# A hybrid short-conv and gated-delta step: the first group prepares the heads' weights ahead of its convolutions

## The chip, the cores and the metric

One Trainium2 chip, one of its cores. The metric is the device time in microseconds (us) of one execution of the whole program. TensorE is called PE here, VectorE DVE, ScalarE ACT, GpSimd POOL, and SyncE, which issues all DMA transfers, SP.

## What is computed

One step of one encoder layer over a prompt of 4096 rows and a sample of 32 rows, 1024 wide:

```python
h    = rmsnorm(x, ln_pre)
proj = h @ w_in          # 4104 columns: B_a | C_a | X_a | Z_a | qkv | Z_g | decay, beta
# group A, 512 channels: short gated conv
y_a  = B_a * conv3_causal(C_a * X_a) * silu(Z_a)
# group B, 4 heads of 128: gated delta rule
q, k, v = silu(conv4_causal(qkv));  q, k L2-normalised
S_t  = exp(g_t) (I - beta_t k_t k_t^T) S_{t-1} + beta_t k_t v_t^T;   o_t = q_t^T S_t / sqrt(dk)
y_g  = rmsnorm_head(o) * silu(Z_g)
y    = x + rmsnorm(concat(y_a, y_g) @ w_out, ln_post)
```

Outputs are y for the prompt and the sample, and the new convolution histories and states of both.

## The kernel before

The prompt is cut into 16 blocks of 256 rows. The program runs in three stages: sixteen groups in which the projection of the heads' columns, their convolutions and the delta rule are computed (to about 1360 us), then the columns of group A for all rows, then the product with `w_out`. Group 0 holds the sample and block 0, and is written by `first_group`; groups 1 to 15 hold one block each.

The columns of `w_in` are taken in tiles of 128, and the tiles in pairs. Tiles 16 to 19 are q, 20 to 23 k, 24 to 27 v, 28 to 31 Z_g, and the 8 columns of tile 32 the gates; group A has 0 to 15. A pair is named here by its first tile. Group 0 takes the eight pairs in the order 20, 22, 16, 18, 24, 26, 28, 30 (`steps`, L857).

Before a pair can be used, its weights are prepared by `prep_b` (L722), which does the following for the two tiles:

- load each tile, 128 x 1024 numbers of 4 bytes, 0.52 MB, from HBM (L205). Tiles 20 and 21 go to buffers of tag `v`, 22 and 23 to buffers of tag `zg`, all the others to the five buffers of tag `xt` (`NXT`, L33), which the rows of x use too;
- multiply by `ln_pre` (L206), on POOL, for tile 20 on DVE; take the absolute value (L208, ACT), sum it over the rows by products with ones (`rL`, PE), and make a power of two for each column out of it (L223, L224, L229, L230, DVE);
- multiply the tile by it (L232, DVE), turn the scales into a column (`ou`, PE; L239, DVE) and scale the convolution's weights `cw` (L732, DVE);
- cut the tile into two halves of 16 bits: the high one on ACT (L728), the low one on POOL, for tile 21 on DVE (L729). With L729 the tile's buffer is free again, and SP can load another into it.

With both halves there, PE projects the sample and block 0 (`pjs_c` and `pj_c`), ACT takes the result out (`us`, `u`), and DVE convolves it (L436: `qks` and `qk`). `pair` does this for one pair of tiles and one block. The norm of x, its transposes and its cut into halves are in `xprep` (L271 to L299); the convolution's old rows of the sample come from `cache_conv_qkv` (L836, copied by DVE in L840 to `hq`).

Behind the convolutions of a block come the decays (L321 to L399) and the matrices of the two chunks (`stage1`), then a triangular substitution, `subst` (L525 to L573): its right side is set up by DVE (L539 to L541), the 31 steps run on POOL for a block of the prompt (`la`, `lt`, from L546 on) and on DVE for the sample (`hllts`), and DVE transposes the result (L556). From group 1 on `prep_a` prepares a pair of group A's weights beside each block: its loads go to the same five buffers, and its L206 is on DVE.

The order on the engines is not written by hand. A scheduler takes every instruction with a priority, the place at which it was written, and sets each engine's order and SP's order of transfers by it and by its own model of time; on the chip each engine, and SP too, works through its list in that order. `first(fn, *a)` runs `fn` with a priority raised by 1500 places, so that what it writes is put ahead of what was written up to 1500 places before it, where its inputs allow:

```python
for si, (kind, c0) in enumerate(steps):
    ...
    for kd_, c_ in steps[:si + 1 + (AH if si >= AS else 0)]:
        ct = (28 if kd_ == "z" else 16) + c_
        if ct not in W:
            prep_b(ct)
```

`AH` is 1 and `AS` 5: up to the step of pair 24 a pair is prepared in its own step, then one step early. Pair 20 is prepared outside this loop.

Of the kernel before, what the change touches and what calls it, by code (L numbers as in the profile page):

```python
# [41 lines left out]
def bc(ap, axis, n):  # L42

    shape = list(ap.shape)
    shape.insert(axis, n)
    return ap.unsqueeze(axis).to_broadcast(shape)
# [3 lines left out]
def hybrid_kernel(  # L50
# [112 lines left out]
    def w_tile(ct):  # L163
        i = 2 * b_order.index(ct)
        return tuple(w_slot(i + x, [P, KT, P], F16, ct) for x in range(2))
# [16 lines left out]
    def te(shape, dtype, tag, bufs=1, nm=""):  # L182
        return pe.tile(shape, dtype, tag=tag, bufs=bufs, name=f"{tag}{nm}")
# [201 lines left out]
    def in_turn(steps):  # L385

        steps = list(steps)
        while steps:
            steps = [s for s in steps if next(s, steps) is None]

    def decays(b):

        C, nch, E3 = b["C"], b["nch"], b["E3"]
        nr = nch * NH
        sfx = "s" if b["s"] else ""
        gB = te([P, nr, C + 1], F32, "gB" + sfx, 1, b["id"])
        dma(gB, b["gd"].unsqueeze(0).to_broadcast([P, nr, C + 1]))
        V.tensor_tensor(E3[:, 0], gB[:, :, C - 1], gB[:, :, C], ALU.subtract)

        def exps():  # L400
            if C < P:
                A.activation(E3[:, 0], E3[:, 0], AF.Exp)
                return A.activation(E3[:C, 1:3], E3[:C, 1:3], AF.Exp)
            return A.activation(E3[:, 0:3], E3[:, 0:3], AF.Exp)
        queued("exp", exps)
        E = gB[:C, :, :C]
        for c in range(nch):
            for i in range(c * NH, (c + 1) * NH):
                V.scalar_tensor_tensor(E[:, i], E[:, i], E3[:C, 3, i:i + 1], mneg[:C, :C], ALU.subtract, ALU.min)
            queued("exp", lambda: A.activation(E[:, c * NH:(c + 1) * NH], E[:, c * NH:(c + 1) * NH], AF.Exp))  # L410
        b["E"] = E
# [37 lines left out]
    def pair(b, kind, c0):  # L449
        n = b["n"]  # L450
        if kind == "z":
            return z_pair(b, c0)
        if kind == "v":
            return qkv_pair(b, c0, b["v"][:, c0 - 8:c0 - 6, :n])
        h0 = c0 % 4
        return qkv_pair(b, c0, b["qk"][:, h0:h0 + 2, 0 if kind == "k" else 1, :n])
# [42 lines left out]
    def stage1(b, c):  # L499
        norm_qk(b, c, 0)  # L500
        norm_qk(b, c, 1)
        gram(b, c)

    def rnorms(b):
        C, nch = b["C"], b["nch"]
        r = te([P, 2, 2, NH], F32, "r", 2, b["id"])[:C, :nch]
        rf = r.rearrange("p c x h -> p (c x h)")
        sf = b["ss"].rearrange("p c x h -> p (c x h)")
        V.tensor_scalar(sf, sf, EPS, None, ALU.add)
        rsqrt(sf, rf)  # L510
        sm = tl([P, 5, 2, NH], F32, "sm", 3, b["id"])[:C, :, :nch]
        rk, rq = r[:, :, 0], r[:, :, 1]
        br, nb_, nbe, cc, c2 = (sm[:, i] for i in range(5))
        V.tensor_tensor(br, b["beta"], rk, ALU.mult)
        V.scalar_tensor_tensor(nb_, br, -1.0, rk, ALU.mult, ALU.mult)
        V.tensor_tensor(nbe, nb_, b["e1"], ALU.mult)
        V.tensor_scalar(cc, rq, P ** -0.5, None, ALU.mult)
        V.scalar_tensor_tensor(c2, cc, 1.0 / P, cc, ALU.mult, ALU.mult)
        b.update(br=br, nb_=nb_, nbe=nbe, cc=cc, c2=c2)
# [190 lines left out]
    def setup_block(b):  # L710
        b["nch"] = b["n"] // b["C"]
        b["qk"] = tl([P, NH, 2, NB1], F32, "qk", 3, b["id"])
        if b["s"]:
            b["v"], b["zg"] = (te([P, NH, NS], F32, x, 1, "s") for x in ("vs", "zgs"))
        else:
            b["v"], b["zg"] = (tl([P, NH, NB1], F32, x, 2, b["id"]) for x in ("v", "zg"))
        b["hist_new"] = te([P, 12, 3], F32, "hists" if b["s"] else "hist", 2 if b["s"] else 3, b["id"])
        b["ss"] = te([P, 2, 2, NH], F32, "ss", 2, b["id"])[:b["C"], :b["nch"]]
        nb = b["C"] // 32
        b["lad"] = dp.tile([2, NH, 4, 32, 32], F32, tag=f"lad{nb}", bufs=2, name=f"lad{b['id']}")[:b["nch"], :, :nb]  # L720
        b["kd"], b["M"], b["at"], b["rec"] = [], [], [], {}

    def prep_b(ct):

        in_turn([scaled((ct, ct + 1))])
        for i, w in enumerate(wa["w"]):
            hi, lo = W[ct + i] = w_tile(ct + i)
            A.activation(hi, w, AF.Copy)  # L728
            (V if ct + i in VLO else G).tensor_tensor(lo, w, hi, ALU.subtract)  # L729
        if ct < 28:  # L730
            c = ct - 16
            V.tensor_tensor(cw[:, :, c:c + 2], cw[:, :, c:c + 2], bc(usc[:, ct:ct + 2], 1, 4), ALU.mult)  # L732
# [67 lines left out]
    def init_hist(b, ct):  # L800

        c = ct - 16
        inv = te([P, 2], I32, "inv", 2, f"{ct}")
        V.tensor_scalar(inv, usc[:, ct:ct + 2].bitcast(I32), -1, float(254 * BIT), ALU.mult, ALU.add)
        V.tensor_tensor(b["hist"][:, c:c + 2], hq[:, :, c:c + 2].rearrange("p j c -> p c j"),
                        bc(inv.bitcast(F32), 2, 3), ALU.mult)
# [63 lines left out]
    def first(fn, *a):  # L870

        with tc.high_priority(1500):
            fn(*a)

    def ends(gen):
        for _ in gen:
            pass
# [20 lines left out]
    def first_group(grp):  # L898

        for b in grp:  # L900
            setup_block(b)
            if b["s"]:
                b["hist"] = te([P, 12, 3], F32, "hists", 2, "i")
                state[1] = te([P, NH, P], F32, "hl", 4, "s0")
                dma(state[1], state_gdn[0, 0].rearrange("h k v -> k h v"))
        for si, (kind, c0) in enumerate(steps):
            if si == 4:
                in_turn([gates(b) for b in grp])
                for b in grp:
                    decays(b)  # L910
            for kd_, c_ in steps[:si + 1 + (AH if si >= AS else 0)]:
                ct = (28 if kd_ == "z" else 16) + c_
                if ct not in W:
                    prep_b(ct)
            if kind != "z":
                init_hist(smp, 16 + c0)
            for b in grp:
                ends(pair(b, kind, c0))
            if si == 6:
                xprep(groups[1][0])  # L920
            if si in (4, 5):
                for b in grp:
                    if si - 4 < b["nch"]:
                        stage1(b, si - 4)
            if si == 5:
                for b in grp:
                    rnorms(b)
                    subst(b)
            if si == 7:
                in_turn([gates(groups[1][0])])  # L930

    prevs = []
    for gi, grp in enumerate(groups):
        b, s0 = grp[-1], 16 * gi
        if gi == 0:
            first_group(grp)
            for p in grp:
                finish(p, s0)
# [452 lines left out]
```

## Time and profile before

| | |
|---|---|
| three runs | 2382.73, 2385.70 and 2390.21 us (median 2385.7) |
| the profiled execution | 2385.77 us, of which the span from the first to the last instruction is 2384.1 us |
| mean granted clock of PE | 0.956 of full speed |
| busy, share of the span | PE 90%, PE's weight load 72%, DVE 66%, ACT 41%, POOL 56% |
| DMA moved | 230.81 MB, 97 GB/s over the span |

The profile is one execution. All times of instructions are in us from the start of its span. A line such as L232 is the line of the kernel; DVE times are shown with what the engine sat idle for just ahead of the instruction, in brackets with what ended that wait.

### The profile page before, as it was taken

The numbers are of one execution on the slowest core, as the hardware profiler recorded it, in microseconds if no ns is written. First come the engines' busy times: TensorE is split into PE (matmuls) and PEld (weight loads), VectorE is DVE, ScalarE is ACT, GpSimd is POOL, SyncE is SP. The second block draws the span as 40 slices with busy tenths as digits, with TensorE's granted clock in tenths as the row PEclk, the third lists the DMA queues.
The fourth block names the chain that finished last, engine by engine and source line by source line (L and its number), as shares of the span: only waits on it lengthen the run. The fifth ranks groups of instructions, "written<-read, shape, count | busy, mean of one in ns | idle before, by whom it ended". The sixth has DMA issues, their size and how long they took to land. (4 is left out here: it accounts for less than half of the span.)

```text
span 2384.1 us, 48173 instructions
## 1 busy us (share of the span) xinstructions
PE 2141.4 (90%) x18626; PEld 1713.9 (72%) x18626; DVE 1564.8 (66%) x3720; ACT 980.3 (41%) x2513; POOL 1333.7 (56%) x1750
## 2 busy tenths in 40 slices
PE   4676989799889988998899999899999999999998
PEld 3465878687778777877778889788888888444443
DVE  4786877677777786767766655656576656455661
ACT  4454655465556555655565411121221121333331
POOL 4435573656675767566776430674467431466763
PEclk9788999899899999999999999999999999999999
DMA  6344341433334243433342425212211122344441
GB/s 125 46 104 92 87 114 48 78 105 97 91 91 111 87 101 87 115 92 95 80 123 72 148 112 182 84 63 71 89 46 54 45 92 88 113 159 145 136 135 72
DMA packets 257198, 230.81 MB, mean 97 GB/s; under 512 B 111576, under 2 KB 196376, under 8 KB 256968
## 3 DMA queue, kind: packets, MB, share of 16 engines
q1 hardware_dynamic: 256968, 227.73, 33.9%
q8 instruction: 146, 2.39, 0.4%
q14 instruction: 84, 0.69, 0.1%
HBM read 133.09 MB, written 76.74 MB: 88 GB/s over the span
## 5 line engine op out<-in xcount | busy, mean ns | idle before, releaser
L74 PEld LDWEIGHTS <-w 128*128 128x128 f16 x6528 | 624.8, 101 | 117.7 <-POOL w L729 16.9
L74 PE MATMUL pj_c<-hhi,w 128*128 128x256 f16 x3072 | 559.6, 282 | 3.0 <-ACT u L430 3.0
L74 PE MATMUL pj_c<-hlo,w 128*128 128x256 f16 x1536 | 433.4, 282 | 0.0
L74 PEld LDWEIGHTS <-w_a 128*128 128x128 f16 x2880 | 269.5, 98 | 48.0 <-issue 16.0
L74 PEld LDWEIGHTS <-opm 128*128 128x128 f16 x1536 | 149.3, 98 | 176.2 <-issue 0.7
L551 POOL TENSOR_TENSOR lt<-lt 128x112 f32<-128x112 f32 (+29 forms) x496 | 235.4, 475 | 37.0
L436 DVE SCALAR_TENSOR_TENSOR qk<-u,cw,qk 128x256 f32<-128x256 f32 x384 | 238.5, 667 | 9.5 <-ACT qk L434 9.1
L550 POOL TENSOR_TENSOR lt<-la,lt 128x112 f32<-128x112 f32 (+29 forms) x496 | 211.6, 427 | 36.2
L74 PE MATMUL pja<-op,w_a 128*128 128x256 f16 x1536 | 190.0, 273 | 3.1 <-DVE w L1034 1.9
L74 PE MATMUL pj_z<-hhi,w 128*128 128x256 f16 x1024 | 187.9, 281 | 0.0
L74 PE MATMUL ga<-op,w_a 128*128 128x256 f16 x1152 | 147.7, 274 | 10.5 <-DVE w L1034 6.7
L74 PE MATMUL pj_z<-hlo,w 128*128 128x256 f16 x512 | 144.0, 281 | 0.0
L74 PE MATMUL pjo<-w_o,opm 128*128 128x512 f16 x528 | 118.5, 379 | 0.0
L137 POOL TENSOR_TENSOR oss<-oss,mhalf 128x2 f32<-128x2 f32 (+1 forms) x17 | 50.0, 2940 | 114.6 <-DVE oss L1280 114.6
L74 PE MATMUL ro<-w_o,opm 128*128 128x512 f16 x504 | 113.4, 379 | 0.0
L74 PE MATMUL go<-w_o,opm 128*128 128x512 f16 x504 | 113.1, 379 | 0.0
L546 POOL TENSOR_TENSOR la<-la,lt 128x1024 f32<-128x1024 f32 x16 | 38.0, 2374 | 126.9 <-DVE lt L541 103.6
L1034 DVE TENSOR_TENSOR w<-pja,w 128x256 f32<-128x256 f32 x152 | 61.7, 420 | 63.6 <-PE pja L74 61.5
L769 ACT ACTIVATE op<-tsc 128x512 f16<-128x512 f32 x48 | 30.2, 630 | 173.0 <-POOL tsc L775 100.0
L750 POOL TENSOR_TENSOR hl<-xtw,hl 128x512 f16<-128x512 f32 x56 | 66.7, 1208 | 61.9 <-ACT hl L749 61.9
L436 DVE SCALAR_TENSOR_TENSOR v<-u,cw,v 128x256 f32<-128x256 f32 x192 | 98.6, 549 | 3.0 <-ACT v L434 2.8
L437 ACT ACTIVATE qk<-qk 128x512 f32<-128x512 f32 x64 | 40.2, 633 | 142.8 <-DVE qk L436 142.8
(650 smaller groups left out, 4791.4 us busy)
## 6 DMA issues: line engine op xcount, KB each, us to landing
xt<-in_x_prompt_dram SPq DMA_DIRECT2D x32, 512.0 KB
mx<-mxd SPq DMA_DIRECT2D x16, 1024.0 KB
op<-hTd SPq DMA_DIRECT2D x30, 512.0 KB
xtw<-in_w_in_dram SPq DMA_DIRECT2D x28, 512.0 KB
wad<-hl SPq DMA_DIRECT2D x56, 256.0 KB
gB<-gd SPq DMA_DIRECT2D x16, 516.0 KB
hTd<-hhi SPq DMA_DIRECT2D x16, 512.0 KB
hTd<-hlo SPq DMA_DIRECT2D x16, 512.0 KB
```

Source lines behind the costliest of these rows:

```text
L74: return self.queue(nc.tensor.matmul(*a, **k))
L137: G.tensor_tensor(y, x, mhalf[:x.shape[0], :x.shape[-1]], ALU.pow)
L436: V.scalar_tensor_tensor(d, u[:, i, j:j + n], cw[:, j, c0 + i:c0 + i + 1], d, ALU.mult, ALU.add)
L437: queued("silu", lambda: A.activation(dst, dst, AF.Silu))
L546: E.tensor_tensor(la, la, bc(rl, 1, 32), ALU.mult)
L550: E.tensor_tensor(tm, bc(la[:, j, j + 1:32], 2, w), bc(lt[:, j, 0:w], 1, r), ALU.mult)
L551: last = E.tensor_tensor(lt[:, j + 1:32, 0:w], lt[:, j + 1:32, 0:w], tm, ALU.subtract)
L750: G.tensor_tensor(hl[:, 1], src, hl[:, 0], ALU.subtract)
L769: A.activation(d[i][0], t, AF.Copy)
L1034: V.tensor_tensor(dst, p, src, ALU.add)
```

## The change

```diff
@@ first_group
             for kd_, c_ in steps[:si + 1 + (AH if si >= AS else 0)]:
                 ct = (28 if kd_ == "z" else 16) + c_
                 if ct not in W:
-                    prep_b(ct)
+                    first(prep_b, ct)
             if kind != "z":
                 init_hist(smp, 16 + c0)
```

No instruction is added or taken away. The preparation of the pairs 22, 16, 18, 24, 26, 28 and 30 gets the raised priority; that of pair 20 does not pass here. The scheduler makes another order of it on all engines up to about the third group, and the same order as before in the second and third stage.

On SP, at the program's start, the loads stood like this (`vw` are tiles 20 and 21, `zgw` 22 and 23, `xtw_628` and `xtw_641` 16 and 17, `xtw_287` the gates' columns, `hls` the state, `hTds` is a write of the sample's x):

```order
L123 DMA lnp<-in_ln_pre_dram 128x8x1
L266 DMA xts_153<-in_x_sample_dram 32x1024
L828 DMA wecst<-in_conv_qkv_w_dram 48x128
L205 DMA vw_183<-in_w_in_dram 128x8x128
L205 DMA vw_196<-in_w_in_dram 128x8x128
L266 DMA xt_0_232<-in_x_prompt_dram 128x1024
```

and now stand like this:

```order
L205 DMA zgw_453<-in_w_in_dram 128x8x128
L205 DMA zgw_466<-in_w_in_dram 128x8x128
L123 DMA lnp<-in_ln_pre_dram 128x8x1
L266 DMA xts_153<-in_x_sample_dram 32x1024
L828 DMA wecst<-in_conv_qkv_w_dram 48x128
L205 DMA vw_183<-in_w_in_dram 128x8x128
```

The two loads of pair 22 went from behind `hls` to the front; a little later the load of tile 16 also passed `hls`, and that of tile 17 the two writes `hTds`.

On POOL the difference at the start is (`L137` is the power of -1/2 in the norm of x, `w_20` the low half of tile 20):

```order
+L206 TENSOR_TENSOR zgw_453<-zgw_453,lnp 128x1024
+L206 TENSOR_TENSOR zgw_466<-zgw_466,lnp 128x1024
 L137 TENSOR_TENSOR xsss<-xsss,mhalf 32x1
 L206 TENSOR_TENSOR vw_196<-vw_196,lnp 128x1024
 L206 TENSOR_TENSOR xtw_287<-xtw_287,lnp 128x8x8
+L206 TENSOR_TENSOR xtw_628<-xtw_628,lnp 128x1024
 L137 TENSOR_TENSOR xss_231<-xss_231,mhalf 128x2
-L206 TENSOR_TENSOR zgw_453<-zgw_453,lnp 128x1024
-L206 TENSOR_TENSOR zgw_466<-zgw_466,lnp 128x1024
-L206 TENSOR_TENSOR xtw_628<-xtw_628,lnp 128x1024
+L206 TENSOR_TENSOR xtw_641<-xtw_641,lnp 128x1024
 L729 TENSOR_TENSOR w_20_221<-vw_183,w_20_220 128x1024
```

The multiplications of pair 22 and of tiles 16 and 17 moved up, past the norm of x of the sample, past that of block 0, and past the low half of tile 20.

On DVE the rows around the scaling of pair 16 (`xtw_628`, `xtw_641`) were before (`qk_318` are block 0's convolutions of pair 20, `qks` the sample's of pair 22):

```order
L436 SCALAR_TENSOR_TENSOR qk_318<-u_4_438,cw,qk_318 128x256 x6
L429 COPY u_6_613<-histi 128x2x3
L223 TENSOR_SCALAR we_627<-rL_626 128x256
L224 TENSOR_SCALAR we_627<-we_627 128x256
L229 TENSOR_SCALAR wu_656<-we_627 1x256
L230 TENSOR_SCALAR we_627<-we_627 128x256
L431 COPY histss<-us_551 128x6
L232 TENSOR_TENSOR xtw_628<-xtw_628,we_627 128x1024
L436 SCALAR_TENSOR_TENSOR qks<-us_551,cw,qks 128x32
L232 TENSOR_TENSOR xtw_641<-xtw_641,we_627 128x1024
```

and are now:

```order
L230 TENSOR_SCALAR we_627<-we_627 128x256
L325 TENSOR_TENSOR gzs<-gzs,dtb 32x4
L328 TENSOR_SCALAR gexs<-gzs 32x4
L323 TENSOR_TENSOR gz_1038<-g_1036 128x16
L232 TENSOR_TENSOR xtw_628<-xtw_628,we_627 128x1024
L232 TENSOR_TENSOR xtw_641<-xtw_641,we_627 128x1024
L327 SCALAR_TENSOR_TENSOR gexs<-gzs 32x4
L239 COPY usc<-ou_661 128x2
L324 TENSOR_TENSOR gz_1038<-gz_1038,ug 128x16
L436 SCALAR_TENSOR_TENSOR qk_318<-u_4_438,cw,qk_318 128x256 x2
```

The scaling of pair 16 stands ahead of the convolutions of pair 20 instead of behind them, and the later pairs likewise, each ahead of the convolutions that it followed. Further on, the two L206 of `prep_a` in group 1 (`xtw_2559`, `xtw_2567`) stood behind L539 to L541 of block 0's substitution on DVE, and now stand ahead of them.

## Rows read from the trace of the kernel before

**Rows 1.** Busy time of each engine by stretch, with PE's granted clock and the DMA rate
```profile
core 0: us, PE busy (x) PEld busy (x) DVE busy (x) ACT busy (x) POOL busy (x), PEclk, DMA share, GB/s
0.00:50.00 50.00, 20.37 (x177) 16.66 (x178) 19.05 (x57) 21.75 (x33) 20.02 (x27) 1.00 0.69 138
50.00:100.00 50.00, 31.93 (x390) 25.91 (x388) 40.34 (x91) 19.82 (x35) 20.73 (x11) 0.73 0.35 52
100.00:150.00 50.00, 34.73 (x391) 28.25 (x390) 43.43 (x124) 28.34 (x66) 26.28 (x18) 0.83 0.34 70
150.00:200.00 50.00, 37.34 (x351) 31.67 (x349) 39.15 (x115) 25.77 (x74) 19.54 (x25) 0.85 0.61 122
200.00:250.00 50.00, 39.67 (x337) 32.80 (x337) 31.82 (x109) 26.62 (x76) 21.94 (x50) 0.84 0.23 62
250.00:300.00 50.00, 48.72 (x500) 42.82 (x498) 40.71 (x105) 30.97 (x78) 30.92 (x57) 1.00 0.37 96
```
**Rows 2.** Groups of instructions, 50 to 150 us: count, busy, mean ns, idle before
```profile
L74 PEld LDWEIGHTS <-w 128*128 128x128 f16 x565 | 39.0, 108 | 27.3 <-POOL w L729 14.4 <-ACT w L728 2.8 <-issue 2.5
L729 POOL TENSOR_TENSOR w<-xtw,w 128x1024 f16<-128x1024 f32 x10 | 21.6, 2169 | 9.1 <-ACT w L728 9.1
L206 POOL TENSOR_TENSOR xtw<-xtw,lnp 128x1024 f32<-128x1024 f32 x9 | 18.8, 2098 | 34.8 <-DMA xtw<-in_w_in_dram 34.8
L436 DVE SCALAR_TENSOR_TENSOR qk<-u,cw,qk 128x256 f32<-128x256 f32 x24 | 17.2, 760 | 5.0 <-ACT qk L434 5.0
L232 DVE TENSOR_TENSOR xtw<-xtw,we 128x1024 f32<-128x1024 f32 x12 | 14.2, 1217 | 0.0
```
**Rows 3.** Waits of SP, 0 to 240 us: total, times, longest
```profile
SPq L205 <- POOL w L729: 68.5, 7, 18.2
```
**Rows 4.** Timeline of SP at the start: start, duration, line, transfer issued
```profile
2.38 1.05 SPq L205 DMA_DIRECT2D vw<-in_w_in_dram  x2
15.78 2.97 SPq L205 DMA_DIRECT2D zgw<-in_w_in_dram  x2
27.51 0.60 SPq L836 DMA_DIRECT2D wecst<-in_cache_conv_qkv_dram  x1
```
**Rows 5.** Timeline of PE: its wait for the sample's old rows
```profile
41.32 0.29 PE L77 MATMUL gcst<-ident,wecst 36*128 36x36 f32 x1 [6.32 <-DMA wecst<-in_cache_conv_qkv_dram]
```
**Rows 6.** Timeline of DVE, 41 to 53 us
```profile
41.64 0.20 DVE L840 COPY hq<-gcst 128x36 f32<-128x36 f32 x1 [10.17 <-PE gcst L77]
...
45.95 4.06 DVE L232 TENSOR_TENSOR zgw<-zgw,we 128x1024 f32<-128x1024 f32 x2
...
51.99 0.17 DVE L431 COPY hist<-u 128x6 f32<-128x6 f32 x1
52.10 2.06 DVE L429 COPY us<-histsi 128x6 f32<-128x6 f32 x1
```
**Rows 7.** Timeline of POOL, 41 to 224 us
```profile
41.02 1.90 POOL L206 TENSOR_TENSOR xtw<-xtw,lnp 128x1024 f32<-128x1024 f32 x1 [6.66 <-DMA xtw<-in_w_in_dram]
...
52.00 2.14 POOL L729 TENSOR_TENSOR w<-zgw,w 128x1024 f16<-128x1024 f32 x1
...
154.85 4.21 POOL L729 TENSOR_TENSOR w<-xtw,w 128x1024 f16<-128x1024 f32 x2 [1.44 <-ACT w L728]
...
187.62 2.68 POOL L546 TENSOR_TENSOR la<-la,lt 128x1024 f32<-128x1024 f32 x1 [7.52 <-DVE lt L541]
...
223.37 0.21 POOL L551 TENSOR_TENSOR lt<-lt 128x8 f32<-128x8 f32 x1
```
**Rows 8.** Timeline of DVE, 196 to 242 us
```profile
202.26 1.23 DVE L206 TENSOR_TENSOR xtw<-xtw,lnp 128x1024 f32<-128x1024 f32 x1 [6.56 <-DMA xtw<-in_w_in_dram]
...
209.08 1.23 DVE L206 TENSOR_TENSOR xtw<-xtw,lnp 128x1024 f32<-128x1024 f32 x1 [5.06 <-DMA xtw<-in_w_in_dram]
...
239.32 0.67 DVE L556 STREAM_TRANSPOSE la<-lt 128x256 f32<-128x256 f32 x1
```
**Rows 9.** Timeline of PE: its longest wait in the second group
```profile
204.08 0.18 PE L74 MATMUL gcs<-g,rev 128*128 128x24 bf16 x1 [10.88 <-DVE g L352]
```

## The prediction

> **What bounds the kernel now.** I read the busy time by stretch first [rows 1]. There the reader sees two regimes. From 250 to 300 us PE is busy 48.72 of 50 us: it sets the pace. Before that it is not: its five busy times add up to 164.0 of 250 us, so 86 us are idle, and they are the only part that a new order of the first group can win back, since the order of the second and third stage is the same. What does the first group wait for? From 50 to 150 us DVE is the fullest engine, 40.34 + 43.43 = 83.8 of 100 us, and so has 16.2 us idle.
>
> Then the groups of instructions for that stretch [rows 2]. The ten L729 on POOL and what PE loads from them belong together: the weight loads of PE stood 27.3 us, 14.4 of them for L729. POOL itself sat 34.8 us ahead of its L206, all of it for loads of weights, and SP held its loads back 68.5 us in seven waits for L729 [rows 3]. This is a loop: L729 frees a buffer, SP loads a tile into it, POOL multiplies it (L206), DVE scales it (L232), and L729 follows. In the order of before the L232 of a pair stands behind the convolutions of the pair ahead of it, so the loop is closed through DVE's longest work; whenever the load then comes late, DVE runs dry. The change opens the loop at that place.
>
> **The change, part by part.** The forecast is a sum against the profiled execution, 2385.77 us, which is also within 0.1 us of the median of the three runs. 0.3% is 7.2 us, about what a measurement of this kernel can tell from no change.
>
> *The start.* The two loads of pair 22 go ahead of everything. They are 1.05 MB, and the first 50 us moved 138 GB/s [rows 1]: 7.6 us by which pair 20's two tiles (issued at 2.38 [rows 4]) and block 0's x arrive later. Three L206 on POOL, of 1.9 us each, also pass the norm of x, but POOL then waits for pair 20's load anyway. Now the cover: DVE stood 10.17 us until 41.64, for the old rows of the sample that PE transposes [rows 6], and PE had stood 6.32 us for their load, `wecst` [rows 5]. Both are later than the whole preparation of pair 20. So a slide of 7.6 us is hidden as long as `wecst`, issued at 27.51 [rows 4], does not slide too. It is queued behind the sample's `hTds` writes, which wait for the sample's norm and so for what has been pushed back, but it also has 1.05 MB fewer right ahead of it. Between ends of 0 (all hidden) and +7.6 (none hidden) I take **+1.4**, near the lower end, because the 10.17 us wait is longer than the slide.
>
> *The pairs.* Each L232 from pair 16 on passes the convolutions of the pair ahead of it: 6 of 0.76 us for one column tile of block 0 [rows 2], and the sample's. Whatever is passed is still done, so nothing is saved by that alone; what can be saved is idle time of DVE. Its 16.2 us between 50 and 150 us are the upper bound, 0 the lower. One wait has nothing to do with weights: 5.0 us for ACT's first product of a convolution (L434) [rows 2]. 16.2 - 5.0 = 11.2, and this I take as the gain: **-11.2**. It is the end nearer to the rows, as the loop's other members have room: the L206 and L729 there take 18.8 + 21.6 = 40.4 of POOL's 100 us [rows 2].
>
> *The shared port.* Filling DVE's pauses has a price. At 52.10 a copy of 6 elements took DVE 2.06 us, beside L729 on POOL from 52.00 for 2.14 us; just ahead of it, at 51.99, a copy of the same shape took 0.17 [rows 6, 7]. So DVE stands still while POOL works on such a tile. In DVE's pauses this cost nothing. If POOL's 40.4 us were spread evenly, 16.2% of them, 6.5 us, fell into pauses, and would now stop DVE: bounds 0 and +6.5. As 11.2 of the 16.2 go, 4.5 is what the even spread would give, and I take somewhat under half of that, **+2.0**, since a POOL operation that runs in such a pause is often the very thing that DVE waits for.
> The Trainium skill, page "SBUF — State Buffer", section "Who interferes with whom", says that VectorE and GpSimd share one pair of ports, as an exclusive lock that whoever starts first holds for the whole instruction. The stretched copy agrees with its 2.06 us. Taken strictly, the rule speaks against this change: every overlap would be paid in full, and the term would be 6.5 instead of 2.0, the sum 4.5 us worse.
>
> *Block 0's substitution and the loads of group 1.* DVE's set-up of the substitution (L541), for which POOL waited 7.52 us before starting at 187.62 [rows 7], now stands behind the two L206 of `prep_a`. These stood 6.56 and 5.06 us for their loads [rows 8]. By the order some 10 us of DVE work lie ahead of the set-up that were behind it, so POOL starts about 10 us later relative to the rest. It ended at 223.6 [rows 7], and DVE fetched the result at 239.32 [rows 8]: 15.7 us to spare. The cover holds, so 0; without it, up to +10. The two L206 now come earlier on DVE, but so do the scalings by which the buffers for their loads come free; their 11.6 us I leave, with 0 for the difference. The longest wait of PE there, 10.88 us at 204.08 [rows 9], for a DVE instruction that runs right behind the first of these L206, stays with them.
>
> *After that.* From 250 us on PE is nearly always busy [rows 1] and passes a shift on one to one; the later stages keep their order. The small swaps in groups 2 and 3 I cost at 0, since they exchange neighbours on engines with pauses.
>
> Sum: 1.4 - 11.2 + 2.0 = -7.8, and 2385.8 - 7.8 = **2378.0 us**.
>
> **The rivals.**
>
> *The late start is not recovered (slower).* If the old rows of the sample land 7.6 us later than at 41.3, DVE's first convolution slides by the whole 7.6 us, and every buffer that L729 frees with it. Block 0's projection cannot start sooner either. The loop is then still fed late, and the idle time only lies elsewhere: I give the pairs nothing, and the ports nothing. 2385.8 + 7.6 = 2393 us. For it: the loads ahead of `wecst` in SP's list wait on work that now starts 7.6 us later. Against it: 10.17 us of slack and the emptier queue. It decides at the moment at which DVE copies `hq`: from about 45 us on it outweighs.
>
> *The lead is given back.* The gain on the pairs is as I say, but the ports take 6.5, and the later set-up of the substitution costs a part of its 10 us, because DVE reaches the L206 earlier than their loads can land: the same 11.2 us of lead, less what the loads gain. With 3 us for that, 1.4 - 11.2 + 6.5 + 3 = -0.3: no change, 2385 us. For it: PE's 10.88 us wait hangs on those loads, and a lead of the engines that the load does not share turns into a longer wait there. Against it: the scalings that free the buffers move with the lead.
>
> *More is won.* If PE's wait of 10.88 us goes too, since the loads of `prep_a` come earlier by more than DVE does, half of it (5.4) is added, and without the port's term and the late start the sum is -11.2 - 5.4 = -16.6: 2369 us. For it: the loads of block 1's x moved forward in SP's list. Against it: the port's row is in the trace.
>
> That the change does nothing of what it says is out: the rows of the order show all seven pairs moved.
>
> **How the numbers follow.** My forecast 0.40, more won 0.22, given back 0.22, late start 0.16. The forecast lies 0.33% below the run of before, so its own spread (2373 to 2383, from the ports' and the start's bounds) falls on both sides of 0.3%: 0.26 faster, 0.14 same. More won is faster, 0.22. Given back is same but for 0.02 on either side, 0.18. Late start is 0.13 slower and 0.03 same. Faster 0.26 + 0.22 + 0.02 = 0.50, same 0.14 + 0.18 + 0.03 = 0.35, slower 0.02 + 0.13 = 0.15. The range reaches from 2366 (more won, with a little to spare for a wait that is not seen) to 2392 (most of the late start): about 0.1 is left out at either end.
>
> **What would show it.** In the trace of the changed kernel: `hq` copied by DVE at 41 to 44 us (the start; at 48 or more the late start is right). L232 of the pairs 16 to 30 each 6 to 16 us earlier than before, and DVE busy about 47 of 50 us from 50 to 100 and close to that up to 140. POOL's idle time ahead of L206 in that stretch clearly under 34.8 us. POOL's substitution of block 0 starting at 187 to 200 us, with L556 not later than at 235. PE's wait ahead of `gcs` between 8 and 14 us. And groups 2 to 15 earlier by the same 7 to 9 us all the way to the end. It would be wrong if `hq` slides; if DVE is full but its short operations are stretched more often; or if block 1 is ahead by 8 us and block 3 is not, as then the steady groups wait for something other than PE.

## The result and the profile after

The changed kernel took 2399.3 us, the median of five runs (2395.4 to 2404.4), beside 2385.7 us before on the same chip (five runs, 2382.7 to 2390.5): 1.0062 of the time before, with an interval of 1.0042 to 1.0082. That is 14.8 us slower (here and below: the ratio less 1, times 2386), on the other side of no change than forecast and beyond the range. Its profiled execution took 2395.4 us, 9.6 more than that of before, over a span of 2393.7 us. Profiled executions lie up to 9 us from their kernel's median here, so a cause needs more than one of them.

The new order reaches further than the first three groups. By the two traces the lists of the engines differ from the start to about 650 us, and again from 913 to 1290 us (groups 10 to 15); elsewhere they are the same. The later stretch cost little: from the first product of block 9's projection (every 384th matmul of the projections in PE's order begins a block) to the end, the change falls back 2.3 us more, and e5, e9, e12, e15 and e17 below, which have its order there, between -1.1 and +0.4. One profile tells this to some 8 us only: the change's own program, run again as e18, falls back 7.7.

The busy times by stretch, with the columns of [rows 1]:

```profile
0.00:50.00 50.00, 13.86 (x132) 11.64 (x133) 12.15 (x43) 17.77 (x27) 17.91 (x26) 1.00 0.62 109
50.00:100.00 50.00, 31.96 (x381) 27.34 (x380) 35.71 (x90) 22.37 (x37) 21.55 (x12) 0.75 0.48 83
100.00:150.00 50.00, 39.76 (x442) 33.01 (x441) 47.41 (x122) 29.61 (x63) 29.04 (x14) 0.84 0.32 66
150.00:200.00 50.00, 37.65 (x372) 32.30 (x370) 28.71 (x90) 26.33 (x79) 9.85 (x10) 0.88 0.68 134
200.00:250.00 50.00, 33.78 (x264) 26.92 (x263) 40.88 (x125) 22.04 (x53) 26.99 (x54) 0.81 0.14 44
250.00:300.00 50.00, 47.88 (x427) 39.17 (x426) 37.00 (x99) 28.50 (x82) 23.81 (x47) 0.91 0.45 98
```

Three things are to be read against [rows 1]. PE starts late: 13.86 us busy in the first 50, where it was 20.37. By 150 us it has made most of that good: 39.76 against 34.73 from 100 to 150 us, with 442 matmuls against 391 recorded. From 200 us on the lead is gone: 33.78 against 39.67, and then 47.88 at a granted clock of 0.91 against 48.72 at 1.00. DVE's pauses were not filled: from 50 to 150 us it is idle 16.9 us, where it was 16.2.

The groups of 50 to 150 us, as in [rows 2]:

```profile
L74 PEld LDWEIGHTS <-w 128*128 128x128 f16 x610 | 44.4, 107 | 19.2 <-issue 6.4 <-POOL w L729 4.3
L729 POOL TENSOR_TENSOR w<-xtw,w 128x1024 f16<-128x1024 f32 x11 | 23.7, 2167 | 2.4 <-ACT w L728 2.4
L206 POOL TENSOR_TENSOR xtw<-xtw,lnp 128x1024 f32<-128x1024 f32 x9 | 21.4, 2375 | 39.7 <-DMA xtw<-in_w_in_dram 39.7
L436 DVE SCALAR_TENSOR_TENSOR qk<-u,cw,qk 128x256 f32<-128x256 f32 x24 | 19.0, 824 | 0.0
L436 DVE SCALAR_TENSOR_TENSOR qks<-us,cw,qks 128x32 f32<-128x32 f32 x24 | 7.0, 334 | 8.5 <-ACT qks L434 8.4
```

The last of them was before:

```profile
L436 DVE SCALAR_TENSOR_TENSOR qks<-us,cw,qks 128x32 f32<-128x32 f32 x18 | 5.5, 350 | 0.4 <-ACT qks L434 0.4
```

The loop was opened in part. The weight loads of PE wait 19.2 us in place of 27.3, 4.3 of them for L729 in place of 14.4. DVE no longer waits ahead of block 0's convolutions (5.0 before), but now 8.5 us ahead of the sample's (`qks`, 0.4 before). The POOL multiplications wait for their loads longer, 39.7 us in place of 34.8. The waits of SP's weight loads for L729 shrank to 59.7 us from 68.5 [rows 3], but a load of x (L266) now waits 16.7 us for it too, which makes 76.4.

The start, on ACT, POOL and PE, and then on DVE (as [rows 6]):

```profile
26.14 1.04 ACT L271 ACTIVATE hhi<-xt 128x1024 bf16<-128x1024 f32 x1
40.65 1.90 POOL L206 TENSOR_TENSOR xtw<-xtw,lnp 128x1024 f32<-128x1024 f32 x1 [6.47 <-DMA xtw<-in_w_in_dram]
42.51 2.12 POOL L729 TENSOR_TENSOR w<-vw,w 128x1024 f16<-128x1024 f32 x1
44.68 0.24 PE L74 MATMUL pjs_c<-hhiss,w 128*128 128x32 f16 x2 [5.32 <-POOL w L729]
47.69 0.69 DVE L285 TENSOR_TENSOR hlo<-gx,hhi 128x512 f16<-128x512 f32 x1 [5.99 <-ACT hhi L284]
49.15 0.18 DVE L840 COPY hq<-gcst 128x36 f32<-128x36 f32 x1
```

The low half of tile 20 on POOL (`w`, L729) was before:

```profile
32.24 2.12 POOL L729 TENSOR_TENSOR w<-vw,w 128x1024 f16<-128x1024 f32 x1
```

`hq` was copied at 49.15, not at 41.64. What came last ahead of it was not `wecst`, for which PE now waited no longer, but the low half of block 0's x (L285), for which DVE waited 5.99 us. The load of x was not what was late: ACT works on its second 128 rows (L271) at 26.14. Their transposes stand on PE behind the sample's products of pair 20, and these waited for the low half of tile 20. On POOL that L729 now stands behind the L206 of tile 17, which waited 6.47 us for its load, and it ran at 42.51 in place of 32.24.

The second group is where the order of SP, DVE, ACT and PE has to be read together. SP, from 180 us on:

```profile
180.99 3.24 SPq L205 DMA_DIRECT2D xtw<-in_w_in_dram  x2
184.34 3.50 SPq L299 DMA_DIRECT2D hTd<-hlo  x1
187.88 4.54 SPq L266 DMA_DIRECT2D xt<-in_x_prompt_dram  x1
192.46 5.12 SPq L497 DMA_DIRECT2D lad<-M  x4
...
204.50 0.79 SPq L536 DMA_DIRECT2D la<-lad  x2
```

DVE in the same stretch, the counterpart of [rows 8]:

```profile
194.48 1.23 DVE L206 TENSOR_TENSOR xtw<-xtw,lnp 128x1024 f32<-128x1024 f32 x1 [10.19 <-DMA xtw<-in_w_in_dram]
201.09 1.22 DVE L206 TENSOR_TENSOR xtw<-xtw,lnp 128x1024 f32<-128x1024 f32 x1 [5.00 <-DMA xtw<-in_w_in_dram]
203.58 0.17 DVE L333 TENSOR_SCALAR gu<-gex 128x16 f32<-128x16 f32 x1
208.58 0.19 DVE L539 TENSOR_SCALAR lt<-la 128x32 f32<-128x32 f32 x1 [0.78 <-DMA la<-lad]
217.59 0.42 DVE L352 TENSOR_TENSOR g<-gsp,g 128x8 bf16<-128x8 f32 x1
```

ACT:

```profile
203.78 0.21 ACT L335 ACTIVATE gsp<-gu 128x8 f32<-128x8 f32 x1 [4.16 <-DVE gu L333]
203.90 0.58 ACT L430 ACTIVATE u<-pj_c 128x512 f32<-128x512 f32 x1
```

PE, with its two waits in this chain (one in [rows 9]), and POOL, as in [rows 7]:

```profile
204.53 0.37 PE L74 MATMUL pj_c<-hhi,w 128*128 128x256 f16 x1 [12.34 <-ACT u L430]
218.06 0.17 PE L74 MATMUL gcs<-g,rev 128*128 128x24 bf16 x1 [4.60 <-DVE g L352]
```

```profile
210.87 2.49 POOL L546 TENSOR_TENSOR la<-la,lt 128x1024 f32<-128x1024 f32 x1 [28.12 <-DVE u L429]
```

Read as one chain: SP issues the loads of tiles 8 and 9 at 181. The matrix of block 0's substitution, whose write (L497) SP could issue at 172.92 before, is ready on DVE 9.3 us later than there, at 182.1; it then stands in SP's list behind those loads, a write and a load of later blocks' x, and is issued at 192.46. DVE waits 10.19 and 5.00 us for the tiles. Behind these two L206 stand block 1's gates (L333 to L352) and the substitution's set-up (L539). The gates' end is at 217.59 in place of 203.87, the substitution's start at 210.87 in place of 187.62. ACT works in order: it cannot copy block 1's projection (L430) before its L335, which waits for DVE's L333. PE waits 12.34 us for that copy and 4.60 us for the gates, where it had one wait of 10.88. The sample's substitution, which DVE itself computes in between, is late too: its result is written out (L564) at 239.28 in place of 223.76.

### The profile page after: what moved, and what is told of

The parts are those of the page before. It is cut to its first block, busy times and chain, and to the rows that moved or that the text cites. A ratio compares the mean times of both kernels' runs of the same rounds, so it can differ in the third digit from the quotient of the medians.

```text
span 2393.7 us, 48188 instructions
## 1 busy us (share of the span) xinstructions
PE 2146.8 (90%) x18626; PEld 1720.1 (72%) x18626; DVE 1552.3 (65%) x3720; ACT 981.6 (41%) x2513; POOL 1334.2 (56%) x1750
## 5 line engine op out<-in xcount | busy, mean ns | idle before, releaser
L74 PEld LDWEIGHTS <-w 128*128 128x128 f16 x6528 | 626.8, 101 | 124.6 <-issue 19.5
L74 PE MATMUL pj_c<-hhi,w 128*128 128x256 f16 x3072 | 569.2, 285 | 18.3 <-ACT u L430 18.3
L550 POOL TENSOR_TENSOR lt<-la,lt 128x112 f32<-128x112 f32 (+29 forms) x496 | 206.6, 417 | 36.3
L74 PE MATMUL pj_z<-hhi,w 128*128 128x256 f16 x1024 | 181.7, 275 | 0.0
L546 POOL TENSOR_TENSOR la<-la,lt 128x1024 f32<-128x1024 f32 x16 | 38.9, 2432 | 157.9 <-DVE lt L541 104.7
L137 POOL TENSOR_TENSOR oss<-oss,mhalf 128x2 f32<-128x2 f32 (+1 forms) x17 | 50.0, 2942 | 114.7 <-DVE oss L1280 114.7
```

The lines of the kernel that those rows point to most:

```text
L74: return self.queue(nc.tensor.matmul(*a, **k))
L137: G.tensor_tensor(y, x, mhalf[:x.shape[0], :x.shape[-1]], ALU.pow)
L546: E.tensor_tensor(la, la, bc(rl, 1, 32), ALU.mult)
L550: E.tensor_tensor(tm, bc(la[:, j, j + 1:32], 2, w), bc(lt[:, j, 0:w], 1, r), ALU.mult)
```

## The experiments

Each was timed in five rounds beside the kernel before on one chip. The table has three marks of each trace, in us from the span's start: DVE's copy of `hq`, the last operation of block 1's gates (L352), and POOL's start of block 0's substitution (L546). All compute the whole output.

| kernel | ratio to before, 95% | us | hq | gates | substitution |
|---|---|---|---|---|---|
| before | 1 | 0 | 41.6 | 203.9 | 187.6 |
| the change | 1.0062 [1.0042, 1.0082] | +14.8 | 49.2 | 217.6 | 210.9 |
| e1_only22 | 1.0034 [1.0018, 1.0051] | +8.1 | 49.6 | 189.4 | 195.5 |
| e4_not22 | 1.0007 [0.9996, 1.0018] | +1.7 | 42.5 | 194.5 | 185.0 |
| e2_p300 | 0.9985 [0.9974, 0.9996] | -3.6 | 50.0 | 205.2 | 187.7 |
| e17_p600 | 1.0039 [1.0024, 1.0054] | +9.3 | 49.9 | 225.9 | 218.3 |
| e3_all1500 | 1.0089 [1.0074, 1.0103] | +21.2 | 45.1 | 216.7 | 210.0 |
| e6_all300 | 0.9982 [0.9969, 0.9996] | -4.3 | 45.2 | 209.8 | 185.8 |
| e7_mix100_200 | 0.9990 [0.9976, 1.0003] | -2.4 | 41.5 | 191.2 | 184.0 |
| e5_la0_ahead | 1.0010 [0.9997, 1.0022] | +2.4 | 48.6 | 222.2 | 203.9 |
| e11_gates_ahead | 1.0041 [1.0024, 1.0058] | +9.8 | 49.6 | 213.0 | 218.0 |
| e12_gates_and_la0 | 0.9979 [0.9964, 0.9994] | -5.0 | 50.3 | 204.0 | 197.5 |
| e8_all1500_la0 | 1.0006 [0.9993, 1.0020] | +1.4 | 44.7 | 222.2 | 204.4 |
| e16_all1500_both_ahead | 0.9960 [0.9945, 0.9975] | -9.5 | 46.2 | 202.4 | 196.1 |
| e14_all300_gates | 1.0001 [0.9985, 1.0016] | 0 | 45.0 | 199.5 | 186.4 |
| e18_stage1_first | 1.0052 [1.0033, 1.0070] | +12.4 | 50.5 | 219.9 | 213.2 |
| e10_before_w8_early | 1.0000 [0.9983, 1.0016] | 0 | 42.1 | 212.4 | 194.3 |
| e13_before_gates | 1.0015 [0.9998, 1.0032] | +3.6 | 41.6 | 194.8 | 186.6 |
| e9_before_la0_behind | 0.9978 [0.9961, 0.9996] | -5.2 | 41.9 | 191.4 | 213.0 |
| e15_before_both_late | 0.9948 [0.9928, 0.9968] | -12.4 | 41.8 | 221.5 | 212.9 |

**Does the start cost by itself?** Only pair 22 keeps the raised priority:

```diff
-                    first(prep_b, ct)
+                    (prep_b if ct != 22 else lambda c: first(prep_b, c))(ct)
```

> Only pair 22 has the precedence, so its two loads stand first in SP's list, and the other pairs are prepared as before; the loads behind block 0's substitution (la0) stand ahead of group 1's weights as before. Theory S (the late start decides): hq is copied at 48 to 50 us instead of 41.64 and the whole is 7 to 10 us slower than before. Theory Q (what decides is that la0 and the set-up of block 0's substitution fell behind the weight loads of group 1): hq slides too, but the time stays within 3 us of before.

Measured 1.0034, +8.1 us, with `hq` at 49.64. That is what the prediction gave for "none hidden" (7.6), but not all of it lies in the start: PE begins block 1's projection 4.8 us later than before and block 3's 10.5 later. The gates are earlier here (189.4), the substitution 7.9 us later (195.5). The converse, all pairs but 22 (`ct == 22` in the same line):

> The precedence for all pairs but 22: pair 20's loads are first as before, the loads of 16 and 17 pass those of 22, the later pairs lead, la0 is ahead of group 1's weight loads. Theories S and Q: -8 to 0 us, what the lead is worth by itself. Rival P (the lead itself costs, as DVE stands still beside POOL and the convolutions come later): 5 us or more slower than before.

Measured 1.0007, no difference, with `hq` at 42.49. But its pairs got little lead (pair 16's L232 at 63.8 in place of 66.2, pair 24's at 99.9 in place of 96.4), so it says little of the lead's price.

**A smaller raise.** All seven pairs, with 300 in place of 1500, then with 600:

```diff
+    def first_p(fn, *a):
+        with tc.high_priority(300):
+            fn(*a)
...
-                    first(prep_b, ct)
+                    first_p(prep_b, ct)
```

> All seven pairs have a precedence of 300 places instead of 1500: pair 22's loads stand first, the pairs lead the convolutions, but la0 stands ahead of group 1's weight loads as before the change. Theory S: as slow as the change, 8 to 13 us above before. Theory Q: within 4 us of before, block 0's substitution starting at 185 to 192 us instead of 210.9. Both in part: some 4 to 7 us above before.

> All seven pairs with 600 places instead of 1500: start, lead, la0 behind group 1's weight loads and the gates behind their L206 as in the change; small differences further on. If those two places, with the change's start and lead, make the loss: 9 to 18 us over before, as the change and the two other runs with both late. If the loss is made of accidents of the order further on: anywhere between 5 us under and 15 over.

At 300: 0.9985, though `hq` is at 50.0, as late as in the change. The gates (205.2) and the substitution (187.7) are where they were before. At 600: 1.0039, with both late. So the start alone does not make the change slow: with the lead, the same late start ends 3.6 us ahead.

**A better start.** The norm's load, the x of the sample and of block 0 and pair 20 get the raise too, of 1500, then of 300; last, 100 for pair 22 and 200 for the others:

```diff
-    xprep(groups[0][0])
+    first(xprep, groups[0][0])
...
-    prep_b(20)
+    first(prep_b, 20)
...
-        xprep(groups[0][1])
+        first(xprep, groups[0][1])
```

> The precedence of the change, given also to ln_pre's load, the norm of x of the sample and of block 0, and pair 20, so that these stand ahead of pair 22 at the start; la0 stays behind group 1's weight loads as in the change. Theory S: hq at 41 to 44 us, and the time at or under that of before (-5 to 0 us). Theory Q: hq as in S, but block 0's substitution starts after 200 us and the time is 8 us or more above before.

> As the run with 300 places, but ln_pre's load, the norm of x of the sample and of block 0, and pair 20 have the 300 places too, so that pair 22's loads stand behind those of pair 20 and of x. hq as in the run with all of the start at 1500 places, 45 us, 5 us earlier than with 300 places alone; la0 early. If the start passes on to the end: 4 to 6 us faster than with 300 places alone, 8 us or so under before. If the lead already hides the start: the same time as with 300 places alone within 2 us.

> Pair 22 with 100 places and the other six with 200: SP's list at the start is that of before, word for word, pair 16 is scaled ahead of pair 20's convolutions, la0 and the set-up of the substitution are ahead of group 1's loads as before. Theories S and Q together: the lead without either of its prices, 6 to 12 us under before. Rival P (the lead is worth little): within 3 us of before.

At 1500 `hq` is 4 us earlier than in the change and the time the worst of all, 1.0089, again with both places of group 1 late. At 300 it is 0.9982, at 100 and 200 0.9990. The last has no late start, and its L232 of the pairs 16, 18, 26 and 28 come 5 to 10 us earlier than before (those of 24 and 30 1 to 5 later). It was expected 6 to 12 us under before, and is no better than e2. So the start and the lead are not two terms that add up: with the lead the late start no longer shows.

**The second group.** Two constraints of order alone undo one place each. The load of tile 8 behind the last of the four loads of block 0's `la` (e5), and the L206 of tiles 8 and 9 behind the end of group 1's gates (e11); e12 has both:

```diff
+            if ct == 8:
+                tc.add_manual_dep(w_ld.ins, LAD["first"][3].ins.name, mybir.DependencyInfo(
+                    mybir.DependencyClass.NoSync, mybir.DependencyReason.DATA), reason="order")
...
+            if ct in (8, 9):
+                tc.add_manual_dep(w_ln.ins, LAD["g3"][2].ins.name, mybir.DependencyInfo(
+                    mybir.DependencyClass.NoSync, mybir.DependencyReason.DATA), reason="order")
```

> The change with one constraint more: on SP the first load of group 1's weights (tile 8) may stand only behind the load la0 of block 0's substitution; the set-up of that substitution then also stands ahead of the two L206 on DVE. The late start stays. Theory Q: la0 is issued some 15 us earlier than in the change (at 185 to 192 us), POOL's substitution starts at 190 to 197 us, and most of the loss goes: 2383 to 2391 us, within 4 us of before. Theory S: the time stays 8 us or more above before.

> The change with one constraint on DVE: the two L206 of group 1's weights may stand only behind the gates of group 1 (the last L352), with la0 as late as in the change. Theory G (DVE waits 10.2 and 5.0 us in these L206 for their loads, ahead of the gates; ACT's logarithm L335 waits for the gates' L333, its copies of PE's projection stand behind that, and PE stops and falls to its lower clock): the 8.4 us that PE loses more than before between 150 and 260 us go for the most part, and the time falls 6 to 12 us against the change, to 0 to 6 us above before. Theory Q (la0's place): no gain, 10 us or more above before.

> The change with both constraints: group 1's weight loads behind la0 on SP, their L206 behind the gates of group 1 on DVE. Theory G: both of PE's losses of 150 to 420 us go, 2380 to 2386 us, at or somewhat under before. Theory Q: as with la0 alone, 1 to 4 us above before.

+2.4, +9.8 and -5.0 us. Undoing the first takes 12.4 us off the change, the second 5.0 (their intervals overlap), both together 19.8. By the traces, every engine's list in e5 and e12 is that of the change up to 181 us, and again from 430 us (e5) and 490 us (e12) on. So the gain comes from the order in between, though more than the two places moved there: of DVE's 3720 instructions some 290 in e12. In e11 the gates no longer stand behind L206, but they still wait: DVE runs a set-up of the substitution (here L544) first, and that waits for its load.

```profile
212.35 0.19 DVE L544 TENSOR_SCALAR lt<-la 128x32 f32<-128x32 f32 x1 [14.70 <-DMA la<-lad]
...
213.03 0.16 DVE L357 TENSOR_TENSOR g<-gsp,g 128x8 bf16<-128x8 f32 x1
```

In e12 DVE waits 9.7 us in these L206, and behind the gates (L360), not ahead of them (L211 is L206 here):

```profile
204.00 0.15 DVE L360 TENSOR_TENSOR g<-gsp,g 128x8 bf16<-128x8 f32 x1
204.73 1.45 DVE L211 TENSOR_TENSOR xtw<-xtw,lnp 128x1024 f32<-128x1024 f32 x1 [0.57 <-DMA xtw<-in_w_in_dram]
215.35 1.23 DVE L211 TENSOR_TENSOR xtw<-xtw,lnp 128x1024 f32<-128x1024 f32 x1 [9.17 <-DMA xtw<-in_w_in_dram]
```

The same constraints on e3 (the first, then both) and the second one on e6:

> The run with all of the start at 1500 places, and the constraint that group 1's weight loads stand behind la0. Theory Q: 14 us or more faster than that run without the constraint (which was 21 us over before), so within 6 us of before. If that run lost its time elsewhere (it fell back a further 8 us in groups 12 to 15): 8 us or more above before.

> The run with all of the start at 1500 places (21 us over before), with both constraints: la0 ahead of group 1's weight loads, the gates ahead of their L206. Theory B: 20 us or more faster than that run without them, 2380 to 2386 us, at or under before. If its loss was elsewhere: 5 us or more over before.

> The run with 300 places for the start and all pairs, with group 1's two L206 behind its gates. Theory G: a further 2 to 5 us less than that run without the constraint, 6 to 10 us under before. If the lead is given back in group 2 and later whatever stands there: the same as without the constraint, 3 to 5 us under before.

From +21.2 to +1.4 and to -9.5 us: 30.7 us for both. But e3 has an order of its own up to 1460 us, which e8 and e16 do not have, and in its profile it falls back 12.4 us from block 9's projection to the end; so not all of the 30.7 need be of the two places. On e6, whose gates were hardly late, the constraint gains nothing. Among the kernels with the lead the time so follows the two places: both late, +9.3 to +21.2 us (the change, e3, e11, e17, and e18, which is the change again); one late, +1.4 and +2.4 (e5, e8); neither, -9.5 to +1.7 (e2, e4, e6, e7, e12, e14, e16). Late means here gates past 212 and a substitution past 209 us; these limits were drawn after the runs.

A further kernel in which both places stay late, with `stage1` at the raised priority as well:

```diff
-                        stage1(b, si - 4)
+                        first(stage1, b, si - 4)
```

> The change, with the precedence of 1500 places for the matrices of block 0's and the sample's chunks (stage1) too: start, lead, la0 behind the weight loads and gates behind the L206 as in the change. If those two places with the change's start and lead make the loss: 9 to 18 us over before. If the loss is made of accidents of the order further on: anywhere between 5 us under and 15 over.

1.0052, with both late. By the traces every engine's list is word for word that of the change, so this is the change timed again: +12.4 beside +14.8 us, marks 1 to 2 us later, and a profiled execution that ends 13.9 us later.

**The same places without the lead.** If a late place has a price of its own, the kernel before must pay it too. `prep_a` of group 1 with the raised priority; the gates ahead of L206; `la`'s first load behind that of tile 9; and that with the gates (L333) behind the L206 of tile 9 as well:

```diff
+            if ct == 9:
+                tc.add_manual_dep(LAD["first"][0].ins, w_ld.ins.name, mybir.DependencyInfo(
+                    mybir.DependencyClass.NoSync, mybir.DependencyReason.DATA), reason="order")
...
+            if ct == 9:
+                tc.add_manual_dep(LAD["gu"][2].ins, w_ln.ins.name, mybir.DependencyInfo(
+                    mybir.DependencyClass.NoSync, mybir.DependencyReason.DATA), reason="order")
```

> The kernel of before with the precedence for group 1's weight pair alone: its loads stand two transposes earlier on SP, la0 still ahead of them, but the first L206 stands ahead of L541 on DVE, the last step of the substitution's set-up. If it is DVE's wait in L206 ahead of the set-up that costs: POOL's substitution starts 6 us or more later than 187.6 and the time is 3 to 8 us over before. If it is the place of la0's load on SP: within 3 us of before.

> The kernel of before with the constraint that group 1's two L206 stand behind its gates; only the first of them stood ahead of the last L352 there, and PE's wait of 10.88 us ahead of gcs hung on it. Theory G: that wait shrinks by 5 us or more, the time is 2 to 6 us under before. If something else is late next: within 2 us of before.

> The kernel of before with one constraint: on SP a part of la0's load stands behind group 1's two weight loads (tiles 8 and 9), so that the set-up of block 0's substitution on DVE also falls behind their two L206, as in the change. Start and pairs as before. Theory Q: the price of that place by itself, 8 to 13 us over before, POOL's substitution of block 0 starting at 200 us or later instead of 187.6. If the place costs only together with the late start or the lead: within 3 us of before.

> The kernel of before, in which both are made late: a part of la0's load behind group 1's weight loads on SP, and group 1's gates on DVE behind the two L206, as in the change; start and pairs as before. Theory B (PE finds work as long as one of the two comes in time, group 1's gates or block 0's substitution; it stops when both are late): gates done at 212 us or later, substitution from 205 us or later, 8 to 16 us over before. If the two places cost only together with the start or the lead of the change: within 4 us of before.

0, +3.6, -5.2 and -12.4 us. That went against the theory: with both places as late as in the change, the kernel before gets faster, and e15, without any change of precedence, has the lowest time of all (its interval overlaps that of e16). Its DVE shows the waits of the change over again:

```profile
201.78 1.22 DVE L211 TENSOR_TENSOR xtw<-xtw,lnp 128x1024 f32<-128x1024 f32 x1 [11.23 <-DMA xtw<-in_w_in_dram]
209.21 1.23 DVE L211 TENSOR_TENSOR xtw<-xtw,lnp 128x1024 f32<-128x1024 f32 x1 [6.02 <-DMA xtw<-in_w_in_dram]
...
212.59 0.19 DVE L551 TENSOR_TENSOR lt<-lt,bl 128x32 f32<-128x32 f32 x1
...
221.51 0.41 DVE L360 TENSOR_TENSOR g<-gsp,g 128x8 bf16<-128x8 f32 x1
```

PE waits there as well, 10.2 us for ACT's copy and 8.2 for the gates, 18.4 together against 16.9 in the change. So these waits by themselves do not make the loss. Two things in e15 are not as in the change: block 0's matrix is ready at 174.3 and not at 182.1, and the sample's substitution is written out at 221.2 and not at 239.3. And the constraints moved more than was asked: from 913 to 1290 us e9 and e15 have the order of the change and not that of before.

The stretches of four kernels, with the columns of [rows 1]. Before:

```profile
0.00:150.00 150.00, 87.03 (x952) 70.82 (x953) 102.81 (x270) 69.92 (x133) 67.04 (x55) 0.85 0.46 87
150.00:260.00 110.00, 87.01 (x782) 72.83 (x779) 80.51 (x248) 58.59 (x161) 45.09 (x76) 0.86 0.41 89
260.00:420.00 160.00, 143.76 (x1400) 125.08 (x1399) 117.02 (x304) 91.28 (x249) 88.77 (x162) 0.95 0.34 87
```

The change:

```profile
0.00:150.00 150.00, 85.58 (x951) 71.99 (x952) 95.28 (x253) 69.75 (x126) 68.50 (x51) 0.86 0.47 86
150.00:260.00 110.00, 81.42 (x691) 67.09 (x689) 77.36 (x240) 56.69 (x156) 40.44 (x76) 0.83 0.43 89
260.00:420.00 160.00, 146.28 (x1391) 125.80 (x1389) 115.70 (x315) 87.45 (x244) 86.75 (x160) 0.93 0.33 84
```

e12:

```profile
0.00:150.00 150.00, 84.31 (x896) 69.89 (x897) 92.19 (x244) 65.40 (x112) 66.64 (x49) 0.83 0.46 82
150.00:260.00 110.00, 89.00 (x804) 74.58 (x805) 80.42 (x261) 64.30 (x183) 56.52 (x82) 0.88 0.39 88
260.00:420.00 160.00, 146.52 (x1458) 128.42 (x1456) 122.08 (x322) 93.56 (x253) 94.92 (x170) 0.98 0.37 92
```

e15:

```profile
0.00:150.00 150.00, 88.82 (x942) 71.48 (x943) 98.91 (x270) 68.93 (x130) 66.21 (x55) 0.85 0.46 87
150.00:260.00 110.00, 84.45 (x731) 71.00 (x730) 75.42 (x232) 57.97 (x159) 43.06 (x76) 0.83 0.39 84
260.00:420.00 160.00, 149.74 (x1481) 130.33 (x1480) 124.57 (x325) 97.22 (x257) 98.40 (x171) 0.97 0.39 92
```

PE's busy time by its granted clock is the work that it did, in us at full speed (rounded clocks leave it uncertain by about 2 over the three rows). Before: 74.0 + 74.8 + 136.6 = 285.4. The change: 73.6 + 67.6 + 136.0 = 277.2. e12: 70.0 + 78.3 + 143.6 = 291.9. e15: 75.5 + 70.1 + 145.2 = 290.8. So by 420 us the change is 8.2 behind, e12 6.5 ahead and e15 5.4 ahead; their profiled executions end 9.6 later, 5.6 and 7.9 earlier. In these, nearly all of each difference has arisen by then. In others it has not: e7 is 8.3 ahead by this count and ends 4.3 later, e8 is 7.6 behind and ends 1.8 earlier, e3 is 8.3 behind and ends 19.2 later. The change loses its 7.2 from 150 to 260 us, at the chain read above. But e15 loses 4.7 there as well, and wins 8.6 from 260 to 420, which the change does not. So the late places need not cost anything by themselves. Why e15 recovers in the next stretch and the change does not, no run here settles; the earlier substitution of the sample is a candidate that was not tested.

## Why the prediction was wrong

*The step that failed* is "Block 0's substitution and the loads of group 1", costed at 0: "The cover holds, so 0", and of the waits for the loads "their 11.6 us I leave". The substitution started 23.2 us later (210.87 against 187.62), not 10, since the prediction moved only its set-up on DVE: the write of its matrix on SP was issued 19.5 us later, 9.3 of them because the matrix itself was ready later, the rest behind the loads of tiles 8 and 9. The two waits of L206 grew from 11.62 to 15.19 us, and the gates, which ended between the two L206 before, now stood behind both. The cover for which the prediction looked held, as POOL ended 5 us ahead of DVE's fetch (L556), but the fetch itself came at 258.00 in place of 239.32. Undoing the two places takes 19.8 us off the change (e12), by the order of 181 to 490 us alone: that term is about +20 here, not 0. Which of the waits carries it stays open, since e15 has them too and gains.

*The start.* Mis-sized: 1.4 forecast, 8.1 in the kernel that has only the late start (e1), 4.8 of them by block 1's projection. The cover counted was the wait for `wecst`; the slide came on another path. The prediction counted the L206 that POOL now does earlier at 1.9 us each, without their waits for loads; the low half of tile 20 stands behind those of tiles 16 and 17, and came 10.3 us later, in e1 11.4. The projection of the sample, and behind it the transposes of x, waited for it.

*The pairs, and the sum without group 1.* A lead there was: PE began block 1's projection 6.6 us earlier. But it did not come out of DVE's pauses, on which the 11.2 us rest. DVE is idle 16.9 us from 50 to 150, where it was 16.2; from 50 to 100 it is busy 35.71 us and not about 47, and by 150 us it has done 7.5 us less than before, 6.9 of them in the first 50. The lead is PE's, whose weight loads wait less for L729. The pairs' L232 came between 5.3 us earlier and 0.7 later, and not 6 to 16 earlier, as the loads, for which POOL waits 39.7 us, did not follow. With group 1 in place, start, lead and port together gave -3.6 (e2) to -5.0 us (e12), where -7.8 was forecast; that this is near is in part luck. The terms do not add up as written: the late start costs up to 8.1 alone and nothing visible beside the lead.

*The shared port.* +2.0 forecast, none seen: from 40 to 230 us DVE had 21 operations on tiles of at most 256 columns stretched over 1 us before, 42.1 us together, and 19 of 38.5 us after, each beside one of POOL.
The rule of the Trainium skill, page "SBUF — State Buffer", section "Who interferes with whom", that the port is held for a whole instruction, agrees with each stretched copy, but the 6.5 us that its strict reading gave are not there either.

*PE "passes a shift on one to one" from 250 us on.* Wrong in part: by the same count the change begins block 3's projection 14.9 us later than before (there at 329.9 us) and ends 9.6 later; e15 begins it 1.0 earlier and ends 7.9 earlier. The fall from 6.6 ahead at block 1 to 14.9 behind at block 3 lies in the groups of the term costed at 0; e12 goes there from 2.2 ahead to 0.2 behind. But e5 falls as far, from 5.1 ahead to 13.9 behind, and is 4.7 behind at the end. The swaps costed at 0 also went on to 650 us and from 913 to 1290 us; from block 9 on no price of theirs shows. Block 1 ahead and block 3 behind was the prediction's own last sign of being wrong.

*The rivals.* The late start had the right sign, its condition held (`hq` at 49.15, past 45 us) and its 2393 us is nearest to the 2399.3 measured. Its mechanism is refuted all the same: the lead was not worth nothing, and e2 and e12 have `hq` at 50 us and gain. "The lead is given back" named the place, a lead turned into a longer wait for the loads of group 1, with a price of 3 us in place of 20.

## What to carry to other kernels

A raised priority of a helper moves its DMA issues on a queue and, through the scheduler, what comes hundreds of instructions later; so follow each moved load past the whole list of its queue, up to the next group, and ask what stands behind the instruction that waits for it on an engine that works in order. When a gain in one place and a loss in the next come in one edit, a constraint of order on the second place (e12, e16) shows them apart, and may be worth more than the edit. Test a place's price in both kernels: undoing it gave 20 us in the one, and putting it into the other came with a gain of 12 (e15). And compare the lists of both programs to their end: a constraint in group 1 moved the order of groups 10 to 15, and one kernel that was to be new (e18) was the old program.

## What the runs showed of the hardware

Behind pauses of PE stand stretches in which it is busy at the lower of its two levels, 1.2 and 2.4 GHz, for a part of the time. In rows of 10 us of the change, with the columns of [rows 1]:

```profile
240.00:250.00 10.00, 8.80 (x80) 6.48 (x78) 3.86 (x15) 7.98 (x28) 3.08 (x9) 0.84 0.07 15
250.00:260.00 10.00, 10.00 (x57) 7.87 (x56) 7.77 (x25) 8.32 (x25) 3.61 (x12) 0.70 0.58 83
...
330.00:340.00 10.00, 7.65 (x88) 5.77 (x85) 7.64 (x23) 3.55 (x9) 6.03 (x4) 0.90 0.17 35
340.00:350.00 10.00, 9.01 (x65) 7.58 (x66) 3.91 (x6) 6.98 (x15) 4.86 (x3) 0.59 0.91 251
```

From 340 to 350 us PE is busy 9.01 us, but at a granted clock of 0.59, 5.3 us at full speed; just ahead, it had been busy 7.65 of 10. From 250 to 260 it is busy all 10.00 at 0.70. So a stretch that looks full in the busy time can hold 30 to 40% less work than at the higher level, and stretches are better compared by the product of both.
